# Attention scores: low-part products in 64 rows of the array, two heads or key halves to one score tile

## The chip, the cores and the metric

The kernel runs on one core of a Trainium2 chip. Its engines are TensorE (PE; its weight loads are listed apart as PEld), VectorE (DVE), ScalarE (ACT), GpSimd (POOL) and SyncE (SP), which issues the DMAs. Time is device microseconds of one execution. Before the change the median of three runs is 2173.24 us.

## The reference

Two layers of an encoder on two groups of tokens ("p": 1024 tokens, "s": 512), D = 1024, heads of 64. Every layer is a normalization, one input projection, three branches (convolution or attention), a gate, and one output projection. The attention parts, each query block of 128:

```python
# layer 0, sliding window of 3 blocks, with a sink
sc = einsum('bnqkgd,bnjkd->bnkgqj', qb, kb) * (d ** -0.5)
p = softmax(concatenate([where(mask, sc, NEG), sink_l], -1), -1)[..., :-1]
# layer 1, axial: 8 query heads on 2 key heads
p = softmax(einsum('bqkgd,bskd->bkgqs', qi, k) * scale, -1)
# layer 1, differential: 4 heads, two scores each
p = softmax(einsum('bqhd,bshd->bhqs', qi, k) * scale, -1).reshape(b, h, 2, 128, s)
a = p[:, :, 0] - lam * p[:, :, 1]
# both layers: 4 heads on 256 memory keys
p = softmax(einsum('bshd,bmhd->bhsm', q, mk) * (d ** -0.5), -1)
```

## The kernel before

**Split numbers.** Every fp32 operand of a product is kept as a high and a low part (fp32r). The projections make three products for each (`mm_a`, L309 to L311, 256 columns; `mm_b`, L323 to L325, 512 columns). Heads have 64 numbers, so q and k of a head are stored with the high parts in rows 0 to 63 and the low parts in rows 64 to 127. `load_q` (L568) makes two tiles: `qhh` with q's high part in both halves, `qll` with its low part in both.

**Scores.** `scores` (L578) makes two products of 128 rows into one PSUM bank: `qhh` by k (high by high and high by low, L579) and `qll` by k (low by high and low by low, L580). The score tiles "s" are a ring of two tiles of one bank, [128, 512] in fp32.

**Softmax.** DVE takes the negative maximum of a score tile (L675, L643 in the window attention), and ACT the exponential with a sum (L677, L650). For 1024 keys `head_softmax` (L681) works on two tiles of 512 keys with a maximum each, and then brings both to one: five small operations on DVE (L694, L696 to L699) and one on ACT (L695). The exponentials are then transposed on PE (128 columns each, four to a "pT" bank; L665, L731, L792, L863), split (`pt_split`), and multiplied by v. `swa` is the window attention (two heads to a step, W = 256 or 384 keys), `ax` the axial one, `diff` the differential one, `mem_attn` the memory one (four query blocks by 256 keys to a head, as two tiles of [128, 2, 256]).

**Order of the work.** The program is written stage by stage: projections of one group, then attention. A scheduler of the framework sets the order of each engine's instructions when the program is built. Attention is marked `urgent` (L189): it is put in as soon as the scheduler holds it ready, and projection products fill the rest of PE's queue. Each engine then runs its own list in that order, and waits where a buffer isn't free. `in_order` makes the slots of a ring go to tiles in program order. The ring "s" also serves the transposes of the first normalizations (`norm_steps(..., "s")`, L918 and L920). Key tiles are a ring of three ("k"), all DMAs go through SP's queue.

Of the kernel before, what the change touches and what calls it, by code (L numbers as in the profile page):

```python
# [45 lines left out]
def in_order(tc, chains):  # L46
    """Slots of a ring go to its tiles in the order of the program: the first writer of each tile is
    scheduled after that of the tile before it."""
# [20 lines left out]
def trunk_kernel(ctx: ExitStack, tc: tile.TileContext, a: dict, dbg=None):  # L69
# [8 lines left out]
    def ring(pool, shape, dt, tag, nm, stream=""):  # L78
        """a tile of a ring whose slots are taken in the order of the program (of its stream)"""
        t = pool.tile(shape, dt, tag=tag, name=nm, bufs=BUFS[tag])  # L80
        chains.setdefault((tag, stream), []).append(t)
        return t
# [27 lines left out]
    # ------------------------------------------------------------ constants  # L110
# [37 lines left out]
    # rotary tables with the gains folded in: cos * g and (signed) sin * g of the other half  # L148
# [14 lines left out]
    # ------------------------------------------------------------ scratch in DRAM  # L163
# [20 lines left out]
    # ------------------------------------------------------------ helpers  # L184
# [10 lines left out]
    def first(f):  # L195
        """what feeds the matrix products of the projections goes before the attention's work"""
        return f
        def g(*args, **kw):
            with tc.high_priority():
                return f(*args, **kw)  # L200
        return g
# [14 lines left out]
    def rstd(out, ss, mul, add):  # L216
        """out = (ss * mul + add) ** -0.5"""
# [71 lines left out]
    def load_act(src, pairs):  # L289
        """pairs of [128, 2, 512], hi and lo, of src [128, n, 512] in DRAM"""  # L290
# [10 lines left out]
    def mm_a(out, hs, sl, w, mid=None):  # L301
        """out[tok, cols] = act[:, sl].T @ w"""
# [12 lines left out]
    def mm_b(out, hs, w, csl, mid=None):  # L315
        """out[cols, tok] = w[:, csl].T @ act"""
# [17 lines left out]
    def stack_now():  # L334
        """the stack of the piece before"""
        while STACK:
            STACK.pop(0)()
# [9 lines left out]
    def between(keep=2):  # L347
        """one step of the work that goes between the projections' products"""
# [5 lines left out]
    def store_stack(t, nh, dst, h0, tok):  # L354
        """t [128, 2, nh, 64] (f32, SBUF): hi and lo, transposed, to dst[:, h0:h0+nh, tok:tok+256]"""
# [18 lines left out]
    def prep(ps, nh, dst, h0, tok, table=None, gain=None, query=False):  # L374
        """a q or k chunk ps [128, 2, nh, 64] (PSUM): rms norm (and a query's HD ** -0.5), gain, rotation"""
# [39 lines left out]
    def put_v(ps, nh, d, dst, t0, tag="stk"):  # L415
        """ps [128, 2, nh, d] (PSUM) to dst[:, 0:nh, t0:t0+2, 0:2d], hi | lo"""
# [10 lines left out]
    def silu2(ps, nm):  # L427
        """2 * silu of ps [128, 512]: ps * (1 + tanh(ps / 2))"""
# [5 lines left out]
    # ------------------------------------------------------------ input projection  # L434
# [9 lines left out]
    def in_proj(g, l, hs, ids, ahead=None, hfs=None):  # L444
        """hfs: the halves of the tokens (all of them if not given)"""
# [71 lines left out]
    def conv_cols(g, c, inner):  # L517
        """0.5 * conv along the tokens of inner; the halves follow one another"""
# [25 lines left out]
    # ------------------------------------------------------------ memory keys and values  # L544
# [22 lines left out]
    # ------------------------------------------------------------ attention  # L567
    def load_q(src, shape):  # L568
        """src(rows) -> AP of 64 rows; the hi rows twice and the lo rows twice"""
# [11 lines left out]

    def pt_split(ps):
# [7 lines left out]
    def fold(o, nm):  # L590
        """rows 64..127 of o [128, n] brought to rows 0..63, SBUF"""
# [5 lines left out]
    def finish_gqa(g, l, o, c0, tok):  # L597
        """o [128, 4, 128]: 4 heads of 128 queries; gated into y's column tiles c0, c0 + 1"""
# [10 lines left out]

    def load_kv(g, l, j):  # L610
        T = GROUPS[g]
        k = ring(sb, [128, 1024], F32R, "k", "k")[:, 0:T]
        dma(out=k, in_=S[g, l, "k", 0][:, j, :])
# [5 lines left out]
    def swa(g, j):  # L619
# [3 lines left out]
        for qt in range(nt):  # L623
# [6 lines left out]
            for hp in range(2):  # L630
# [3 lines left out]
                ss = []  # L634
                for i in range(2):
                    s = ring(psum, [128, 512], F32, "s", "s")[:, 0:W]
                    scores(s, [x[:, 2 * hp + i, :] for x in q2], k[:, b0 * 128:b1 * 128])
                    for side, cond, c0 in ((0, qt > 0, 0), (1, qt < nt - 1, W - 128)):
                        if cond:
                            nc.vector.tensor_tensor(  # L640
                                out=s[:, c0:c0 + 128], in0=s[:, c0:c0 + 128], in1=wmask[:, side, :], op=ALU.add
                            )
                    nc.vector.tensor_reduce(out=nm[:, i:i + 1], in_=s, axis=AXL.X, op=ALU.max, negate=True)  # L643
                    ss.append(s)
# [4 lines left out]
                for i in range(2):  # L649
                    nc.scalar.activation(  # L650
                        out=e[:, i, :], in_=ss[i], func=ACTF.Exp, bias=nm[:, i:i + 1], accum_out=su[:, i:i + 1],
# [21 lines left out]
    def softmax(s, e, su, nm):  # L673
        """s [128, n, w] (PSUM): nm [128, n] = -max, e [128, n, w] = exp(s + nm), su [128, n] the sums"""
# [6 lines left out]
    def head_softmax(q2, k, T, e):  # L681
        """one head, 128 queries: e [128, T]: exp(scores - max), with the max of each 512 columns;
        the result [128, T / 512]: what each 512 columns are to be multiplied by"""
        n = T // 512
        nm, su = smalla(n, "nm"), smalla(n, "su")
        for i in range(n):
            s = ring(psum, [128, 1, 512], F32, "s", "s")
            scores(s[:, 0, :], q2, k[:, i * 512:(i + 1) * 512])
            softmax(s, e[:, i * 512:(i + 1) * 512].unsqueeze(1), su[:, i:i + 1], nm[:, i:i + 1])
        if n == 1:  # L690
            nc.vector.reciprocal(out=su, in_=su)
            return su
        mn, f = smalla(1, "sk"), smalla(n, "sx")
        nc.vector.tensor_tensor(out=mn, in0=nm[:, 0:1], in1=nm[:, 1:2], op=ALU.min)  # L694
        nc.scalar.activation(out=f, in_=nm, func=ACTF.Exp, bias=mn, scale=-1.0)  # L695
        nc.vector.tensor_tensor(out=su, in0=su, in1=f, op=ALU.mult)  # L696
        nc.vector.tensor_tensor(out=mn, in0=su[:, 0:1], in1=su[:, 1:2], op=ALU.add)
        nc.vector.reciprocal(out=mn, in_=mn)
        nc.vector.tensor_tensor(out=f, in0=f, in1=mn.to_broadcast([128, n]), op=ALU.mult)  # L699
        return f  # L700

    @urgent
    def ax(g, j):
        T = GROUPS[g]
        nt = T // 128
        per = 1024 // T
        k, v = load_kv(g, 1, j)
        for qt in range(nt):
# [3 lines left out]
            for hp in range(2):  # L712
                es = []
                for i in range(2):
                    if i % per == 0:
                        e2 = et("e")
                    e = e2[:, (i % per) * T:(i % per + 1) * T]
                    h = 4 * j + 2 * hp + i
                    f = head_softmax([x[:, 2 * hp + i, :] for x in q2], k, T, e)
                    for n in range(T // 512):  # L720
                        c = e[:, n * 512:(n + 1) * 512]
                        nc.gpsimd.tensor_scalar(
                            out=c, in0=c, scalar1=f[:, n:n + 1], scalar2=0.5, op0=ALU.mult, op1=ALU.mult
# [383 lines left out]
```

## Time and profile before

| | |
|---|---|
| three runs | 2166.95, 2173.24, 2174.95 us |
| profiled execution, span from first to last instruction | 2165.8 us (the page gives no other time of it) |
| mean granted TensorE clock | 0.988 |
| busy: PE, PEld, DVE, ACT, POOL | 96%, 88%, 71%, 55%, 50% |
| score products on PE | 1024: 320 + 320 of 512 keys, 64 + 64 of 384, 128 + 128 of 256 |

PE's rows give a start and a length for each product. Products overlap, so what one costs in a full queue is the distance from its start to the next start, not its length. The distances are read from the timeline.

### The profile page before, as it was taken

What the parts mean: (1) busy time and instruction counts of PE and PEld (TensorE: products, weight loads), DVE (VectorE), ACT (ScalarE), POOL (GpSimd) and SP (SyncE); (2) the same over time, 40 slices, a digit from 0 to 9 for tenths busy, and PEclk for the clock granted to TensorE, in tenths of its full rate; (3) what the DMA queues carried; (4) which work ended last, traced back from release to release, by engine and by line L of the source; (5) the groups of instructions that cost most, each with busy time, mean ns of one, the idle gap of its engine ahead of it and who ended that gap; (6) DMA issues with size and microseconds to landing.
All of it is one profiled execution on the core that took longest, in us unless ns stands there. A gap on an engine that the chain in (4) does not pass through costs nothing. (4 is left out here: it accounts for less than half of the span.)

```text
span 2165.8 us, 41192 instructions
## 1 busy us (share of the span) xinstructions
PE 2080.9 (96%) x14336; PEld 1916.8 (88%) x14336; DVE 1547.2 (71%) x3264; ACT 1189.7 (55%) x2838; POOL 1075.9 (50%) x1134
## 2 busy tenths in 40 slices
PE   6999999999999999999999989997998999999999
PEld 6988978889999999999998878886997899998999
DVE  8768877745445687877988886777778877875652
ACT  5545633453334566766766655546466666764441
POOL 6845532342225674853855574332346686842331
PEclk9999999999999999999999999998999999999999
DMA  6675463436776522443345565447475566567753
GB/s 229 193 214 169 140 210 106 115 100 212 250 234 220 174 84 88 131 129 114 94 121 180 165 194 166 122 147 229 143 213 179 167 186 203 175 204 217 227 169 105
DMA packets 317408, 363.74 MB, mean 168 GB/s; under 512 B 25360, under 2 KB 222736, under 8 KB 317200
## 3 DMA queue, kind: packets, MB, share of 16 engines
q1 hardware_dynamic: 317200, 361.10, 54.6%
q8 instruction: 114, 1.87, 0.4%
q14 instruction: 94, 0.77, 0.1%
HBM read 261.38 MB, written 99.61 MB: 167 GB/s over the span
## 5 line engine op out<-in xcount | busy, mean ns | idle before, releaser
L187 POOL TENSOR_TENSOR wlo<-wraw,whi 128x512 fp32r<-128x512 f32 x182 | 249.3, 1371 | 322.9 <-ACT whi L186 285.0
L186 ACT CAST whi<-wraw 128x512 fp32r<-128x512 f32 x388 | 237.3, 621 | 254.8 <-PE po L311 74.9
L677 ACT ACTIVATE e<-s,nm 128x512 f32<-128x512 f32 (+1 forms) x416 | 264.4, 640 | 173.4 <-DVE nm L675 124.5
L675 DVE TENSOR_REDUCE nm<-s 128x1 f32<-128x512 f32 (+1 forms) x368 | 248.0, 681 | 37.7 <-PE s L580 36.2
L587 DVE TENSOR_TENSOR ptlo<-pT,pthi 128x512 fp32r<-128x512 f32 x352 | 238.0, 683 | 42.6 <-ACT pthi L586 40.9
L586 ACT CAST pthi<-pT 128x512 fp32r<-128x512 f32 x352 | 201.1, 588 | 118.1 <-PE pT L665 48.4
L309 PE MATMUL po<-whi,ahi 128*128 128x256 f32 x896 | 254.7, 285 | 1.7 <-DVE xr L900 1.4
L310 PE MATMUL po<-wlo,ahi 128*128 128x256 f32 x896 | 254.0, 284 | 0.0
L311 PE MATMUL po<-whi,alo 128*128 128x256 f32 x896 | 253.5, 284 | 0.5 <-DVE alo L187 0.4
L187 DVE TENSOR_TENSOR wlo<-wraw,whi 128x512 fp32r<-128x512 f32 x206 | 175.9, 855 | 105.1 <-ACT whi L186 104.4
L309 PE MATMUL pa<-whi,ahi 128*128 128x256 f32 x768 | 221.2, 288 | 4.0 <-DVE z L431 2.1
L311 PE MATMUL pa<-whi,alo 128*128 128x256 f32 x768 | 221.3, 288 | 0.0
L310 PE MATMUL pa<-wlo,ahi 128*128 128x256 f32 x768 | 221.2, 288 | 0.0
L223 POOL TENSOR_TENSOR rs<-ss,mhalf 128x8 f32<-128x8 f32 (+2 forms) x108 | 141.7, 1313 | 149.7 <-DVE ss L219 141.6
L579 PE MATMUL s<-k,qhh 128*128 128x512 f32 (+2 forms) x512 | 194.6, 385 | 17.2 <-ACT e L677 10.6
L580 PE MATMUL s<-k,qll 128*128 128x512 f32 (+2 forms) x512 | 185.5, 367 | 2.6 <-DMA qll<-st_p1dq 1.6
L309 PEld LDWEIGHTS po<-whi,ahi 128*128 128x128 f32 x896 | 171.1, 191 | 3.7 <-DVE xr L900 1.8
L311 PEld LDWEIGHTS po<-whi,alo 128*128 128x128 f32 x896 | 171.1, 191 | 2.0 <-DVE alo L187 0.9
L310 PEld LDWEIGHTS po<-wlo,ahi 128*128 128x128 f32 x896 | 171.3, 191 | 1.3
L324 PE MATMUL pb<-h,whi 128*128 128x512 f32 x432 | 171.6, 397 | 0.0
L325 PE MATMUL pb<-h,wlo 128*128 128x512 f32 x432 | 171.4, 397 | 0.0
L323 PE MATMUL pb<-h,whi 128*128 128x512 f32 x432 | 170.9, 396 | 0.0
(171 smaller groups left out, 6272.9 us busy)
## 6 DMA issues: line engine op xcount, KB each, us to landing
wraw<-in_w_in_dram SPq DMA_DIRECT2D x252, 256.0 KB, 3.1
wraw<-in_w_out_dram SPq DMA_DIRECT2D x120, 256.0 KB, 3.4
alo<-y_p SPq DMA_DIRECT2D x20, 512.0 KB, 5.0
zg_p<-z SPq DMA_DIRECT2D x32, 256.0 KB, 3.0
k<-st_p1dk SPq DMA_DIRECT2D x14, 512.0 KB, 4.4
v<-dv_p SPq DMA_DIRECT2D x14, 512.0 KB, 5.4
zg<-zg_p SPq DMA_DIRECT2D x48, 128.0 KB, 2.7
y_p<-yo SPq DMA_DIRECT2D x48, 128.0 KB, 2.6
```

The costliest lines, as they stand in the source:

```text
L186: nc.scalar.copy(out=out_hi, in_=src)
L187: lo_eng.tensor_tensor(out=out_lo, in0=src, in1=f32(out_hi), op=ALU.subtract)
L309: nc.tensor.matmul(out=out, lhsT=h, rhs=wh, start=(k == 0), stop=False)
L310: nc.tensor.matmul(out=out, lhsT=h, rhs=wl, start=False, stop=False)
L311: nc.tensor.matmul(out=out, lhsT=l_, rhs=wh, start=False, stop=(k == n - 1))
L324: nc.tensor.matmul(out=out, lhsT=wh, rhs=l_, start=False, stop=False)
L579: nc.tensor.matmul(out=out, lhsT=q2[0], rhs=k, start=True, stop=False)
L580: nc.tensor.matmul(out=out, lhsT=q2[1], rhs=k, start=False, stop=True)
L586: nc.scalar.copy(out=hi, in_=ps)
L587: nc.vector.tensor_tensor(out=lo, in0=ps, in1=f32(hi), op=ALU.subtract)
L675: nc.vector.tensor_reduce(out=nm, in_=s, axis=AXL.X, op=ALU.max, negate=True)
L677: nc.scalar.activation(out=e[:, j, :], in_=s[:, j, :], func=ACTF.Exp, bias=nm[:, j:j + 1], accum_out=su[:, j:j + 1],)
```

## The change

- `scores2` fills one score tile of two banks, [128, 2, 512], one bank for each of two heads (window attention, and the 512-token group) or for each half of 1024 keys. It makes two products of 128 rows with `qhh` as before, then two products of 64 rows: q's low part by k's high part, the first in rows 0 to 63, the second in rows 64 to 127 of the array. The products of low by low parts are left out.
- For the second one, k's high part must lie in rows 64 to 127. `load_k` with `swap` loads the two halves of k the other way round, in two DMAs. The window attention now takes two tiles of the ring "k" for a key head, where it took one; for 1024 keys one tile holds the first half as stored and the second half swapped. The program issues 1604 DMAs, where it issued 1556.
- The ring "s" has one tile, of two banks, where it had two of one bank.
- A score tile has one maximum over [128, 2, W], [128, 1024] or [128, 2, 512], and the window's mask is added for both heads at once. For 1024 keys the five small operations on DVE and the one on ACT go, and one reciprocal of [128, 1] is left.
- `mem_attn` keeps its 128-row products, with one score tile [128, 4, 256] to a head.

```diff
-    "s": 2, "t": 2, "x": 1, "d": 2, "o": 1,
+    "s": 1, "t": 2, "x": 1, "d": 2, "o": 1,
...
+    def scores2(s, qs, ks):
+        for i in range(2):
+            nc.tensor.matmul(out=s[:, i, :], lhsT=qs[i][0], rhs=ks[i], start=True, stop=False)
+        for i in range(2):
+            r = slice(64 * i, 64 * i + 64)
+            nc.tensor.matmul(out=s[:, i, :], lhsT=qs[i][1][r], rhs=ks[i][r], start=False, stop=True)
+
+    def load_k(k, src, swap):
+        if not swap:
+            dma(out=k, in_=src)
+            return
+        for r in range(2):
+            dma(out=k[64 * r:64 * r + 64], in_=src[64 - 64 * r:128 - 64 * r])
...
+    def load_k2(src, T):
+        k = ring(sb, [128, 1024], F32R, "k", "k")
+        load_k(k[:, 0:512], src[:, 0:512], False)
+        load_k(k[:, 512:1024], src[:, T - 512:T], True)
+        return k[:, 0:512], k[:, 512:1024]
...
     def load_kv(g, l, j):
         T = GROUPS[g]
-        k = ring(sb, [128, 1024], F32R, "k", "k")[:, 0:T]
-        dma(out=k, in_=S[g, l, "k", 0][:, j, :])
+        src = S[g, l, "k", 0][:, j, :]
+        if l:
+            k = load_k2(src, T)
+        else:
+            k = []
+            for i in range(2):
+                k.append(ring(sb, [128, 1024], F32R, "k", "k")[:, 0:T])
+                load_k(k[i], src, i == 1)
...
-                ss = []
-                for i in range(2):
-                    s = ring(psum, [128, 512], F32, "s", "s")[:, 0:W]
-                    scores(s, [x[:, 2 * hp + i, :] for x in q2], k[:, b0 * 128:b1 * 128])
...
-                    nc.vector.tensor_reduce(out=nm[:, i:i + 1], in_=s, axis=AXL.X, op=ALU.max, negate=True)
-                    ss.append(s)
+                s = ring(psum, [128, 2, 512], F32, "s", "s")[:, :, 0:W]
+                scores2(
+                    s, [[x[:, 2 * hp + i, :] for x in q2] for i in range(2)],
+                    [x[:, b0 * 128:b1 * 128] for x in k],
+                )
+                for side, cond, c0 in ((0, qt > 0, 0), (1, qt < nt - 1, W - 128)):
+                    if cond:
+                        nc.vector.tensor_tensor(
+                            out=s[:, :, c0:c0 + 128], in0=s[:, :, c0:c0 + 128],
+                            in1=wmask[:, side, :].unsqueeze(1).to_broadcast([128, 2, 128]), op=ALU.add,
+                        )
+                nc.vector.tensor_reduce(out=nm, in_=s, axis=AXL.X, op=ALU.max, negate=True)
...
-    def head_softmax(q2, k, T, e):
-        n = T // 512
-        nm, su = smalla(n, "nm"), smalla(n, "su")
-        for i in range(n):
-            s = ring(psum, [128, 1, 512], F32, "s", "s")
-            scores(s[:, 0, :], q2, k[:, i * 512:(i + 1) * 512])
-            softmax(s, e[:, i * 512:(i + 1) * 512].unsqueeze(1), su[:, i:i + 1], nm[:, i:i + 1])
-        if n == 1:
-            nc.vector.reciprocal(out=su, in_=su)
-            return su
-        mn, f = smalla(1, "sk"), smalla(n, "sx")
-        nc.vector.tensor_tensor(out=mn, in0=nm[:, 0:1], in1=nm[:, 1:2], op=ALU.min)
-        nc.scalar.activation(out=f, in_=nm, func=ACTF.Exp, bias=mn, scale=-1.0)
-        nc.vector.tensor_tensor(out=su, in0=su, in1=f, op=ALU.mult)
-        nc.vector.tensor_tensor(out=mn, in0=su[:, 0:1], in1=su[:, 1:2], op=ALU.add)
-        nc.vector.reciprocal(out=mn, in_=mn)
-        nc.vector.tensor_tensor(out=f, in0=f, in1=mn.to_broadcast([128, n]), op=ALU.mult)
-        return f
+    def two_softmax(qs, ks, es):
+        n = len(es)
+        s = ring(psum, [128, 2, 512], F32, "s", "s")
+        scores2(s, qs, ks)
+        sv = s.rearrange("p a k -> p (a k)").rearrange("p (n k) -> p n k", n=n)
+        nm, su = smalla(n, "nm"), smalla(n, "su")
+        nc.vector.tensor_reduce(out=nm, in_=sv, axis=AXL.X, op=ALU.max, negate=True)
+        for j in range(n):
+            nc.scalar.activation(
+                out=es[j], in_=sv[:, j, :], func=ACTF.Exp, bias=nm[:, j:j + 1], accum_out=su[:, j:j + 1],
+            )
+        nc.vector.reciprocal(out=su, in_=su)
+        return [su[:, j:j + 1] for j in range(n)]
+
+    def softmax_pair(q2s, kk, T):
+        if T == 1024:
+            es = [et("e") for _ in range(2)]
+            fs = []
+            for i in range(2):
+                fs += two_softmax([q2s[i]] * 2, kk[i], [es[i]])
+        else:
+            eb = et("e")
+            es = [eb[:, i * T:(i + 1) * T] for i in range(2)]
+            fs = two_softmax(q2s, [kk[i][i] for i in range(2)], es)
+        return es, fs
...
-                    for t2 in range(0, 4, 2):
-                        s = ring(psum, [128, 2, 256], F32, "s", "s")
-                        for t in range(2):
-                            scores(s[:, t, :], [x[:, (t2 + t) * 128:(t2 + t + 1) * 128] for x in q2], k2[:, i, :])
-                        qt = 4 * qb + t2
-                        softmax(s, e[:, t2:t2 + 2, :], su[:, t2:t2 + 2], smalla(2, "nm"))
+                    s = ring(psum, [128, 4, 256], F32, "s", "s")
+                    for t in range(4):
+                        scores(s[:, t, :], [x[:, t * 128:(t + 1) * 128] for x in q2], k2[:, i, :])
+                    softmax(s, e, su, smalla(4, "nm"))
```

The scheduler makes a new order. Three places of it follow.

**PE, axial attention, group p.** `s` is a score tile, `pa` a projection of 256 columns, `o` the product with v. Before, with two products to each tile of 512 keys:

```order
L579 MATMUL s<-k,qhh 128x512
L580 MATMUL s<-k,qll 128x512
L310 MATMUL pa<-wlo,ahi 128x256
L311 MATMUL pa<-whi,alo 128x256
L309 MATMUL pa<-whi,ahi 128x256
L579 MATMUL s<-k,qhh 128x512
L580 MATMUL s<-k,qll 128x512
```

and in the changed kernel, where L587 are the 128-row products and L590 those of 64 rows:

```order
L311 MATMUL pa<-whi,alo 128x256
L309 MATMUL pa<-whi,ahi 128x256
L587 MATMUL s<-k,qhh 128x512 x2
L590 MATMUL s<-k,qll 128x512 x2
L310 MATMUL pa<-wlo,ahi 128x256
```

The four products of 1024 keys now stand together. From L590 here to the next L587, 36 rows on, the order has 34 products of 256 columns and 8 transposes. Of the 208 pairs of 64-row products, 198 stand side by side like this; in the other 10 something stands between the two.

**PE, memory attention of layer 0, group s.** `pT` are transposes, `o` the product with v of 512 columns. Before, two tiles that follow each other:

```order
L579 MATMUL s_18726<-k_18702,qhh_18709 128x256
L580 MATMUL s_18726<-k_18702,qll_18712 128x256
L865 MATMUL o_18616<-pthi_18622,v_18580 128x512
L579 MATMUL s_18774<-k_18702,qhh_18766 128x256
L580 MATMUL s_18774<-k_18702,qll_18769 128x256
...
L865 MATMUL o_18616<-ptlo_18623,v_18580 128x512
```

and in the changed kernel, the end of one tile (L579 and L580 are its last two of eight products) and the start of the next:

```order
L579 MATMUL s_17515<-k_17446,qhh_17507 128x256
L580 MATMUL s_17515<-k_17446,qll_17510 128x256
L891 MATMUL pT_17482<-ident_r_66,e_17459 128x128
L891 MATMUL pT_17493<-ident_r_66,e_17459 128x128
...
L893 MATMUL o_17481<-pthi_17487,v_17448 128x512
L893 MATMUL o_17481<-ptlo_17488,v_17448 128x512
L893 MATMUL o_17481<-pthi_17498,v_17448 128x512
L893 MATMUL o_17481<-ptlo_17499,v_17448 128x512
L579 MATMUL s_17579<-k_17564,qhh_17571 128x256
```

Between two tiles of two banks stand the eight transposes and four products of the head before, and nothing of a projection.

**DVE, axial attention.** Before, the small operations of one head, and the maximum that follows:

```order
L694 TENSOR_TENSOR sk<-nm 128x1
L696 TENSOR_TENSOR su<-su,sx 128x2
L697 TENSOR_TENSOR sk<-su 128x1
L698 RECIPROCAL sk<-sk 128x1
L699 TENSOR_TENSOR sx<-sx,sk 128x2
L675 TENSOR_REDUCE nm<-s 128x1
```

and now, with L721 the maximum over 1024 keys and L726 the reciprocal:

```order
L388 TENSOR_TENSOR raw<-raw,rs 128x512
L721 TENSOR_REDUCE nm<-s 128x1
L726 RECIPROCAL su<-su 128x1
L605 TENSOR_TENSOR ptlo<-pT,pthi 128x512 x2
L721 TENSOR_REDUCE nm<-s 128x1
```

The five small operations between two maxima became one.

## Rows read from the trace of the kernel before

**Rows 1.** The page: its first line and the busy time of each engine.

```profile
span 2165.8 us, 41192 instructions
PE 2080.9 (96%) x14336; PEld 1916.8 (88%) x14336; DVE 1547.2 (71%) x3264; ACT 1189.7 (55%) x2838; POOL 1075.9 (50%) x1134
```

**Rows 2.** What TensorE (PE) waited for: total us, times, longest us.

```profile
PE s L579 <- ACT e L677: 10.6, 11, 2.4
```

**Rows 3.** Two stretches: span, busy us of each engine (xcount), granted clock, DMA share, GB/s.

```profile
756.00:810.00 54.00, 54.00 (x395) 50.62 (x394) 46.18 (x104) 36.49 (x88) 40.71 (x46) 1.00 0.28 84
1458.00:1512.00 54.00, 42.03 (x209) 33.11 (x209) 40.09 (x98) 35.65 (x100) 12.82 (x22) 0.87 0.78 227
```

**Rows 4.** The largest group of PE's low-part score products.

```profile
L580 PE MATMUL s<-k,qll 128*128 128x512 f32 x320 | 128.6, 402 | 1.6 <-DMA qll<-st_p1dq 1.6
```

**Rows 5.** PE in order of time in an axial stretch: start us, us, instruction.

```profile
835.86 0.60 PE L731 MATMUL pT<-ident_r,e 128*128 128x128 f32 x4
836.21 0.36 PE L310 MATMUL pa<-wlo,ahi 128*128 128x256 f32 x1
836.41 0.28 PE L311 MATMUL pa<-whi,alo 128*128 128x256 f32 x1
836.53 0.28 PE L309 MATMUL pa<-whi,ahi 128*128 128x256 f32 x1
...
838.39 0.40 PE L579 MATMUL s<-k,qhh 128*128 128x512 f32 x1
838.62 0.40 PE L580 MATMUL s<-k,qll 128*128 128x512 f32 x1
838.86 0.28 PE L311 MATMUL pa<-whi,alo 128*128 128x256 f32 x1
```

**Rows 6.** PE in order of time in a sliding-window stretch.

```profile
322.38 0.34 PE L580 MATMUL s<-k,qll 128*128 128x384 f32 x1
322.55 0.40 PE L324 MATMUL pb<-h,whi 128*128 128x512 f32 x1
```

**Rows 7.** PE's weight loads (PEld) in order of time, axial stretch.

```profile
838.27 0.19 PEld L579 LDWEIGHTS s<-k,qhh 128*128 128x128 f32 x1
838.39 0.19 PEld L580 LDWEIGHTS s<-k,qll 128*128 128x128 f32 x1
```

**Rows 8.** Groups on VectorE (DVE), shapes kept apart.

```profile
L675 DVE TENSOR_REDUCE nm<-s 128x1 f32<-128x512 f32 x320 | 216.1, 681 | 32.4 <-PE s L580 31.3
L643 DVE TENSOR_REDUCE nm<-s 128x1 f32<-128x384 f32 x64 | 33.7, 547 | 0.5
L696 DVE TENSOR_TENSOR su<-su,sx 128x2 f32<-128x2 f32 x128 | 35.1, 274 | 35.6 <-ACT sx L695 25.9 <-ACT e L677 9.5
```

**Rows 9.** One score tile in the axial stretch and the next in its bank.

```profile
837.68 0.39 PE L580 MATMUL s<-k,qll 128*128 128x512 f32 x1
838.11 0.69 DVE L675 TENSOR_REDUCE nm<-s 128x1 f32<-128x512 f32 x1 [0.26 <-PE s L580]
838.90 0.69 ACT L677 ACTIVATE e<-s,nm 128x512 f32<-128x512 f32 x1 [0.61 <-DVE nm L675]
839.48 0.19 ACT L677 ACTIVATION_READ_ACCUMULATOR e<-s,nm 128x1 f32 x1
...
842.38 0.48 PE L579 MATMUL s<-k,qhh 128*128 128x512 f32 x1
```

**Rows 10.** PE in the memory attention: first products of the first and the eighth tile.

```profile
1479.49 0.56 PE L579 MATMUL s<-k,qhh 128*128 128x256 f32 x1 [0.22 <-ACT e L650]
...
1493.55 0.36 PE L579 MATMUL s<-k,qhh 128*128 128x256 f32 x1
```

**Rows 11.** ACT there: two exponentials of one tile.

```profile
1485.39 0.49 ACT L677 ACTIVATE e<-s,nm 128x256 f32<-128x256 f32 x1
1485.86 0.48 ACT L677 ACTIVATE e<-s,nm 128x256 f32<-128x256 f32 x1
```

**Rows 12.** DMA issues of one kind of key tile: count, KB each, median us to landing.

```profile
k<-st_p1dk SPq DMA_DIRECT2D x14, 512.0 KB, 4.4
```

More of the change, by code (lines that the diff above doesn't have):

```diff
@@ L633, in swa @@
                 ns = nsink[:, h0:h0 + 2]
-                ss = []
-                for i in range(2):
-                    s = ring(psum, [128, 512], F32, "s", "s")[:, 0:W]
-                    scores(s, [x[:, 2 * hp + i, :] for x in q2], k[:, b0 * 128:b1 * 128])
[L638 to L642, printed above, removed]
-                    nc.vector.tensor_reduce(out=nm[:, i:i + 1], in_=s, axis=AXL.X, op=ALU.max, negate=True)
-                    ss.append(s)
+                s = ring(psum, [128, 2, 512], F32, "s", "s")[:, :, 0:W]
[10 more added lines that the diff above has]
+                nc.vector.tensor_reduce(out=nm, in_=s, axis=AXL.X, op=ALU.max, negate=True)
                 nc.vector.tensor_tensor(out=nm, in0=nm, in1=ns, op=ALU.min)
@@ L650, in swa @@
                     nc.scalar.activation(
-                        out=e[:, i, :], in_=ss[i], func=ACTF.Exp, bias=nm[:, i:i + 1], accum_out=su[:, i:i + 1],
+                        out=e[:, i, :], in_=s[:, i, :], func=ACTF.Exp, bias=nm[:, i:i + 1], accum_out=su[:, i:i + 1],
                     )
@@ L705, in ax @@
         nt = T // 128
-        per = 1024 // T
         k, v = load_kv(g, 1, j)
@@ L712, in ax @@
             for hp in range(2):
[L713 to L721, printed above, removed]
+                es, fs = softmax_pair([[x[:, 2 * hp + i, :] for x in q2] for i in range(2)], [k, k], T)
+                for e, f in zip(es, fs):
+                    for c in (e[:, n * 512:(n + 1) * 512] for n in range(T // 512)):
                         nc.gpsimd.tensor_scalar(
-                            out=c, in0=c, scalar1=f[:, n:n + 1], scalar2=0.5, op0=ALU.mult, op1=ALU.mult
+                            out=c, in0=c, scalar1=f, scalar2=0.5, op0=ALU.mult, op1=ALU.mult
                         )
-                    es.append(e)
                 for kc in range(nt // 2):
@@ L746, in diff @@
         nt = T // 128
-        per = 1024 // T
         ks = []
         for i in range(2):
-            k = ring(sb, [128, 1024], F32R, "k", "k")[:, 0:T]
-            dma(out=k, in_=S[g, 1, "dk", hd // 2][:, 2 * (hd % 2) + i, :])
-            ks.append(k)
+            src = S[g, 1, "dk", hd // 2][:, 2 * (hd % 2) + i, :]
+            if T == 1024:
+                ks.append(load_k2(src, T))
+            else:
+                k = ring(sb, [128, 1024], F32R, "k", "k")[:, 0:T]
+                load_k(k, src, i == 1)
+                ks.append((k, k))
         vs = []
@@ L767, in diff @@
                 qt = 2 * qp2 + t
-                e2, fs = [], []
-                for i in range(2):
-                    if i % per == 0:
-                        eb = et("e")
-                    e = eb[:, (i % per) * T:(i % per + 1) * T]
-                    fs.append(head_softmax(
-                        [x[:, i, t * 128:(t + 1) * 128] for x in q2], ks[i], T, e,
-                    ))
-                    e2.append(e)
+                e2, fs = softmax_pair(
+                    [[x[:, i, t * 128:(t + 1) * 128] for x in q2] for i in range(2)], ks, T
+                )
                 for n in range(T // 512):
@@ L779, in diff @@
                     nc.gpsimd.tensor_scalar(
-                        out=c1, in0=c1, scalar1=fs[1][:, n:n + 1], scalar2=lamb, op0=ALU.mult, op1=ALU.mult
+                        out=c1, in0=c1, scalar1=fs[1], scalar2=lamb, op0=ALU.mult, op1=ALU.mult
                     )
                     nc.vector.scalar_tensor_tensor(
-                        out=c0, in0=c0, scalar=fs[0][:, n:n + 1], in1=c1, op0=ALU.mult, op1=ALU.subtract
+                        out=c0, in0=c0, scalar=fs[0], in1=c1, op0=ALU.mult, op1=ALU.subtract
                     )
```

## The prediction

> **What bounds the kernel now.** I read the page's busy times first, then what PE waits for, then the stretches, then the products one by one. PE is busy for 2080.9 of 2165.8 us; no other engine comes over 71%, if PE's own weight loads are left aside [rows 1]. Its idle time is 84.9 us in all, and the score products' wait for a free bank is a small part of it: 10.6 us in 11 waits [rows 2]. The stretches show two regimes. In the axial stretch PE has no idle time at all, because projection products lie between the pieces of attention; in the stretch from 1458 us, where attention has little projection work beside it, PE is busy for 42.0 of 54 us and its mean granted clock falls to 0.87 [rows 3]. So almost everywhere a microsecond of PE's queue that goes is a microsecond of the kernel, and in a few tens of microseconds the length of the attention's own chain counts instead.
>
> What a product costs is the distance between starts: 0.12 us for 256 columns and 0.23 to 0.24 for 512 [rows 5], 0.17 for 384 [rows 6]. The record of a 512-column product is 0.40 us long [rows 4, 5], so about 0.17 us of it lies under the next one.
>
> **The change, part by part.**
>
> *Low-part products.* Of the 512 low-part products, 96 belong to the memory attention and stay. The other 416 become 208 pairs: 160 of 512 columns, 32 of 384, 16 of 256. If the two of a pair run at the same time, a pair costs one distance instead of two. At best the second starts with the first: 160 x 0.235 + 32 x 0.17 + 16 x 0.12 = 45.0 us saved. At worst, if they overlap, the second starts one weight load behind the first; weight loads stand 0.12 us apart [rows 7], which leaves 160 x 0.115 + 32 x 0.05 + 0 = 20.0 us. No row shows two products at once, so nothing tells where between these it lies; I take the middle, 32.5 us. Ten of the 208 pairs have other work between their products and are counted as lost: 32.5 x 198/208 = 31 us, all of it on the path, since it is PE's queue.
>
> The Trainium skill, "TensorE: Matmul & The Clock Gate", section "Measured speedup vs the span model", says that products in different row groups start some 4 ns apart. By that page the saving would be about 44 us, and the time, as an estimate, 2136 us instead of the 2149 below; no run here shows it yet.
>
> *The switch between 128-row and 64-row products.* Each pair needs one switch there and one back, 416 in all; the trace has none. The nearest thing in it is the switch between transposes and products. Four transposes and the product behind them take 0.55 us from the first start to the start after (835.86 to 836.41); with 0.12 for the product that leaves 0.11 for each transpose, no more than a weight load [rows 5, 7]. That switch costs nothing that can be seen, so I take 0. The other end is an array that must run empty first: 0.17 us, the part of a record that otherwise lies under the next product, and 0.12 more if the weight load has to wait too. A gain from the switch I can exclude, since it adds a condition and removes no work. This end is a rival below.
>
> *One score tile where there were two.* The next tile's first product now waits for the last exponential of the tile before it. Rows 9 show what one tile takes: 1.99 us from its last product's start (837.68) to the end of its exponential (839.67), and its bank is used again 2.71 us later. For 1024 keys the maximum grows with its columns, 0.134 us for each 128 (from 0.547 to 0.681 us [rows 8]), to 1.22 us, 0.54 more; and a second exponential of 0.77 us follows [rows 9]. That is 3.3 us. The new order puts 34 products of 256 columns and 8 transposes between two tiles there: 34 x 0.12 + 8 x 0.11 + 0.235 = 5.2 us. The wait is covered with 1.9 us to spare.
>
> It isn't covered in the stretch from 1458 us. In the memory attention eight tiles start within 14.06 us [rows 10], seven steps, so 4.0 us to a head. One tile to a head makes a chain: eight products (0.84 us to the last start), 0.3 until the maximum, 1.22, 0.1, four exponentials 0.47 us apart [rows 11] for 1.9, and 0.1: 4.5 us, of which nothing overlaps with the next head's. That is 0.5 us for each of four heads, 2 us at least. The ceiling comes from the whole new order, priced with the distances above: 24 of the 231 gaps between tiles hold under 4 us of PE work, nearly all of them in this stretch; if each were filled up to 4 us with waiting it would be 49 us, of which some 12 are idle time that is already there [rows 3], so 37. I take 6, near the lower end, because the window attention held both its banks until its last exponential before, too.
>
> *The start.* The first sixteen transposed blocks of the normalizations pass through the same ring, now one tile at a time, each held for one 512-column operation of DVE, about 0.68 us [rows 8]. If all were exposed it would be 11 us. DVE does its next step on the same block meanwhile, and PE's transposes fit in beside that; I take 1.
>
> *DVE and ACT.* For each of 128 heads' blocks, five small operations of about 0.27 us [rows 8] become one reciprocal, and two maxima become one: some 1.1 + 0.15 us of 128 x 1.25 = 160 us, a tenth of DVE's time. DVE isn't the bound, so I count 0. If PE's waits shorten with it, that would be a gain of up to 10 us, an eighth of PE's idle time.
>
> *Loads of k.* 48 DMAs more in SP's queue. A key tile lands 4.4 us after its issue [rows 12] and is issued a stage ahead. In the window attention two of the ring's three tiles now belong to one key head, so the second head's second copy is loaded only when the first head is done. Projection work covers that in group p: 0. Without cover it costs one landing for each such head, two heads, 9 us, in the high end.
>
> **Sum.** The profiled execution spans 2165.8 us, and the page gives no other time of it; the median of the three runs is 7.4 us above that, 0.3%. Against the median: 2173.2 - 31 + 6 + 1 = **2149 us**, 1.1% less. The measurement tells about 0.5% from no change, 11 us here: 2162 and 2184 are the marks.
>
> **The rivals.**
>
> *The switch empties the array.* Every one of the 416 switches then costs 0.17 us on PE: 71 us, and the time is 2149 + 71 = 2220; with the weight loads waiting too, 50 us more, 2270. This turns the sign once a switch costs over 24/416 = 0.058 us, a third of what the record leaves. For it: the 64-row products use another division of the array, which the transposes don't. Against it: the transposes' switch is free [rows 5]. The Trainium skill, "TensorEngine Tiling (Array Packing)", section "Key Properties", says just this: changing the tiling mode drains TensorE. By that page this rival would be the forecast, and no run here shows it yet. Chance 0.27.
>
> *The pairs don't overlap.* The second 64-row product waits for the first, as any product does today. Then nothing is saved, and 2173 + 7 = 2180 us. Speaking for it: there isn't one pair of products in this trace that ran at once. Chance 0.12.
>
> *The single score tile binds.* The waits of the thin stretch come out near their ceiling, with part of the start exposed: 30 to 48 us instead of 7, so 2172 to 2190. For it: PE already idles for 12 us there, and waits for DVE and ACT queue behind other work. Against it: the slack of 1.9 us elsewhere, and less work on DVE. Chance 0.13.
>
> *The forecast*, pairs overlap at a cheap switch: 0.48, with its own range from 2126 (45 us saved, waits as now, and a few us from DVE) to 2165.
>
> **How the numbers follow.** Faster by over 0.5%: the forecast but for its upper edge, 0.46. Within 0.5%: that edge 0.02, most of the pairs that don't overlap 0.09, most of the single tile 0.08, a switch of 0.06 to 0.08 us 0.02: 0.21. Slower: the dearer switches 0.25, and 0.08 from the other two: 0.33. The range goes from 2126, the best pairs, to 2224, the emptied array with its 0.17 us; beyond lie the dearer switch, 0.09, and some 0.09 more on both sides.
>
> **What would show it.** In PE's timeline of the changed kernel: L590's second product at most 0.12 us behind the first, the next 128-row product 0.23 us behind the second, and no gap between the last L587 and the first L590 beyond 0.24. A gap of 0.4 or more at both borders is the emptied array; 0.23 between the two L590 is no overlap. Waits of L587 on ACT's exponential far over today's 10.6 us, outside the thin stretch too, are the single tile. The maximum should read 1.2 us, and DVE's busy time some 1390 us. I would be wrong altogether if PE's idle time grew outside these places, by the new order alone.

## The result and the profile after

The changed kernel takes 2237.75 us (median of 4 runs, 2237.17 to 2242.96), the kernel before 2170.09 in the same comparison: a ratio of 1.032, 95% interval 1.0296 to 1.0344. It is 68 us slower, where 2149 us, 1.1% less, had been forecast. The page of the changed kernel, to be held against [rows 1]:

```profile
span 2235.4 us, 39938 instructions
PE 2141.3 (96%) x14336; PEld 1882.8 (84%) x14336; DVE 1422.1 (64%) x2408; ACT 1135.5 (51%) x2454; POOL 1086.4 (49%) x1134
```

DVE and ACT got relief (125 and 54 us less busy), and no gain of it shows. PE makes the same 14336 products and is busy 60 us longer; its idle time is 94.1 us after 84.9. So of the 70 us by which the span grew, most lies in how long the products take. PE's timeline shows one pair of 512 columns (start us, us, instruction, count of products in the row):

```profile
803.03 0.61 PE L587 MATMUL s<-k,qhh 128*128 128x512 f32 x2
803.58 0.50 PE L590 MATMUL s<-k,qll 64*128 64x512 f32 x2
804.01 0.50 PE L323 MATMUL pb<-ahi,whi 128*128 128x512 f32 x1
804.35 0.40 PE L324 MATMUL pb<-alo,whi 128*128 128x512 f32 x1
804.58 0.39 PE L325 MATMUL pb<-ahi,wlo 128*128 128x512 f32 x1
```

The two 64-row products of L590 lie in 0.50 us together: they start 3 ns apart (median of the 153 pairs of 512 columns that stayed together), so they do overlap. But both borders are dear. From the second L587 (0.22 behind the first) to the pair it takes 0.33 us instead of 0.23, from the pair to the next 128-row product 0.43, and from that to the one after it 0.34. PE's weight loads of the same pair show what goes with the last one:

```profile
803.58 0.18 PEld L590 LDWEIGHTS s<-k,qll 64*128 64x128 f32 x2 [0.35 <-issue]
804.01 0.19 PEld L323 LDWEIGHTS pb<-ahi,whi 128*128 128x128 f32 x1 [0.24 <-issue]
804.11 0.19 PEld L324 LDWEIGHTS pb<-alo,whi 128*128 128x128 f32 x1
```

Elsewhere a weight load stands one product ahead of its product [rows 5, 7]; L323's at 804.01 comes with it, and L324's only 0.11 us later. Over all pairs the medians say the same: 0.09 us too much going in, 0.20 coming out, 0.11 behind, 0.40 us for the round trip (into the 64-row division of the array and back), against 0.23 saved by the overlap (512 columns). That is a loss of 0.17 us for each of 160 pairs, and by the same medians 0.23 for 32 pairs of 384 columns and 0.28 for 16 of 256: 39 of the 68 us.

The largest piece of the rest shows in one stretch. PE's groups of lines from 1485 to 1555 us (columns: instruction and count | busy us, mean ns | idle us before) hold attention alone; not one projection product stands among them. Three of them:

```profile
L697 PE MATMUL pT<-ident_r,e 128*128 128x128 f32 x40 | 10.0, 382 | 0.7 <-DVE yo L854 0.6 <-DVE e L688 0.2
L587 PE MATMUL s<-k,qhh 128*128 128x256 f32 (+2 forms) x18 | 6.6, 459 | 7.7 <-ACT e L682 6.1 <-ACT e L723 1.6
L579 PE MATMUL s<-k,qhh 128*128 128x256 f32 x16 | 6.3, 404 | 2.1 <-ACT e L682 1.6 <-ACT e L709 0.5
```

The same stretch as a window (span, busy us of PE, PEld, DVE, ACT, POOL, granted clock, DMA share, GB/s), and before's stretch without projection products:

```profile
1485.00:1555.00 70.00, 50.66 (x199) 35.12 (x200) 47.06 (x114) 31.82 (x96) 13.86 (x22) 0.71 0.51 141
```

```profile
1471.00:1506.00 35.00, 24.83 (x113) 18.88 (x113) 23.62 (x57) 20.99 (x66) 9.54 (x19) 0.80 0.89 248
```

Without filling, PE is busy 7 us in 10, and the clock falls to its lower level, 1.2 GHz, for part of the time. This bare stretch was 36 us long before (from the end of the last projection product to the next one's start) and is 71 us long now. In both kernels the same 6348 projection products stand ahead of it, but of PE's other products 3015 instead of 3130: more attention is left for it. The changed kernel comes to it 14 us later than the kernel before and leaves it 49 us later. The mean granted clock of the whole execution went from 0.988 to 0.978.

### The profile page after: what moved, and what is told of

The parts are those of the page before. It is cut to its first block, busy times and chain, and to the rows that moved or that the text cites. A ratio compares the mean times of both kernels' runs of the same rounds, so it can differ in the third digit from the quotient of the medians.

```text
span 2235.4 us, 39938 instructions
## 1 busy us (share of the span) xinstructions
PE 2141.3 (96%) x14336; PEld 1882.8 (84%) x14336; DVE 1422.1 (64%) x2408; ACT 1135.5 (51%) x2454; POOL 1086.4 (49%) x1134
## 4 chain that ended last, share of the span: by engine, by line
PE 81%; DMA 7%; DVE 5%; ACT 2%; issue 2%; POOL 2%; SPq 0%; ACTq 0%; POOLq 0%; DVEq 0%
PE pb L323 7%; PE pb L325 7%; PE pb L324 7%; PE pa L309 7%; PE pa L310 7%; PE pa L311 6%; PE po L309 4%; PE po L311 4%; PE po L310 4%; PE s L587 4%; PE s L590 4%; PE o L768 4%; PE pT L764 3%; PE stT L366 2%; PE pT L822 1%
## 5 line engine op out<-in xcount | busy, mean ns | idle before, releaser
L723 ACT ACTIVATE e<-s,nm 128x1024 f32<-128x1024 f32 (+1 forms) x192 | 186.5, 973 | 189.1 <-DVE nm L721 182.4
L605 DVE TENSOR_TENSOR ptlo<-pT,pthi 128x512 fp32r<-128x512 f32 x352 | 233.5, 684 | 76.7 <-ACT pthi L604 74.9
L604 ACT CAST pthi<-pT 128x512 fp32r<-128x512 f32 x352 | 196.6, 590 | 132.2 <-PE pT L697 52.7
L721 DVE TENSOR_REDUCE nm<-s 128x1 f32<-128x1024 f32 (+1 forms) x160 | 194.9, 1218 | 68.2 <-PE s L590 67.4
L756 POOL TENSOR_SCALAR e<-e,su 128x512 f32<-128x512 f32 x160 | 121.1, 770 | 142.7 <-DVE su L726 136.4
L324 PE MATMUL pb<-h,whi 128*128 128x512 f32 x432 | 172.5, 399 | 0.0
L323 PE MATMUL pb<-h,whi 128*128 128x512 f32 x432 | 172.4, 399 | 0.0
L309 PE MATMUL pa<-whi,h 128*128 128x256 f32 x576 | 165.8, 288 | 0.4 <-ACT raw L377 0.4
```

What stands on the lines that cost most here:

```text
L309: nc.tensor.matmul(out=out, lhsT=h, rhs=wh, start=(k == 0), stop=False)
L323: nc.tensor.matmul(out=out, lhsT=wh, rhs=h, start=(k == 0), stop=False)
L324: nc.tensor.matmul(out=out, lhsT=wh, rhs=l_, start=False, stop=False)
L604: nc.scalar.copy(out=hi, in_=ps)
L605: nc.vector.tensor_tensor(out=lo, in0=ps, in1=f32(hi), op=ALU.subtract)
L721: nc.vector.tensor_reduce(out=nm, in_=sv, axis=AXL.X, op=ALU.max, negate=True)
```

## The experiments

All ratios are to the kernel before in the same comparison, with 95% intervals.

### The tile alone

```diff
-        for i in range(2):
-            nc.tensor.matmul(out=s[:, i, :], lhsT=qs[i][0], rhs=ks[i], start=True, stop=False)
-        for i in range(2):
-            r = slice(64 * i, 64 * i + 64)
-            nc.tensor.matmul(out=s[:, i, :], lhsT=qs[i][1][r], rhs=ks[i][r], start=False, stop=True)
+        for i in range(2):
+            scores(s[:, i, :], qs[i], ks[i])
```

and k loaded as before, in one DMA.

> The single score tile of two banks with its one maximum, the changed order of the rest and the joined exponentials, but every score product over 128 array rows and k loaded unswapped in one DMA. Theory A (a round trip between the 128-row and the 64-row division costs 0.40 us against 0.23 us that the pair saves, so 39 us come from the pairs, and the other 28 from the single tile and the lower clock behind it): about 2198 us, 2187 to 2210, with windows of the thin stretch (from 1458 us) again below 46 us of PE time. Theory B (all 68 us come from the borders of the pairs): 2170, within 0.5% of before. Theory C (all come from the single tile and the order, the pairs are neutral): 2238.

Measured: 2198.42 us, ratio 1.014 (1.0097 to 1.0182). Theory A's number. The page:

```profile
span 2199.1 us, 39942 instructions
PE 2096.1 (95%) x14336; PEld 1927.0 (88%) x14336; DVE 1418.7 (65%) x2408; ACT 1129.7 (51%) x2454; POOL 1096.2 (50%) x1134
```

The tile costs some 29 us and the pairs the other 39 (2237.75 less 2198.42); the interval leaves 21 to 39 us for the tile. That the pairs' 39 us are also what the distances gave is partly chance: against this run the changed kernel's PE is busy 45 us longer and idle 9 us less, and its bare stretch is longer too. The same products as in the kernel before now leave PE idle for 103.0 us, 18 more, and the bare stretch is 54 us long.

### The pair alone

```diff
-    "s": 1, "t": 2, "x": 1, "d": 2, "o": 1,
+    "s": 2, "t": 2, "x": 1, "d": 2, "o": 1,
...
-            nc.tensor.matmul(out=s[:, i, :], lhsT=qs[i][1][r], rhs=ks[i][r], start=False, stop=True)
+            nc.tensor.matmul(out=s[i], lhsT=qs[i][1][r], rhs=ks[i][r], start=False, stop=True)
```

with two one-bank tiles, and the maxima and rescaling of before.

> The products of the low parts in pairs of 64 rows, but into two score tiles of one bank each as in the kernel before, with a maximum per 512 keys, the small rescaling operations and the memory heads of before. Theory A: about 2209 us, 2197 to 2222 (before plus 160 x 0.171 + 32 x 0.23 + 16 x 0.278 = 39 us). Theory B: 2238. Theory C: 2139 to 2170, since the pairs would then save 31 us or nothing.

Measured: 2298.04 us, ratio 1.0591 (1.0552 to 1.0629). No theory gave that, since the edit did more than was meant. With two tiles the scheduler pulled the couples apart; in PE's timeline one 64-row product stands alone:

```profile
832.60 0.48 PE L587 MATMUL s<-k,qhh 128*128 128x512 f32 x1
833.01 0.50 PE L590 MATMUL s<-k,qll 64*128 64x512 f32 x1
833.43 0.50 PE L325 MATMUL pb<-ahi,wlo 128*128 128x512 f32 x1
```

Only 28 of 208 pairs stayed together, and there are 388 round trips instead of 218. PE's busy time rose by 149 us over before, 0.38 us to a round trip, though the run couldn't isolate the pair. In this program it was the single tile that kept the pairs together.

### The same rows, and a single switch

In the changed kernel, both products in rows 0 to 63 (k loaded unswapped), and apart from that the order of the four products:

```diff
-            r = slice(64 * i, 64 * i + 64)
+            r = slice(0, 64)
```

```diff
         for i in range(2):
             nc.tensor.matmul(out=s[:, i, :], lhsT=qs[i][0], rhs=ks[i], start=True, stop=False)
-        for i in range(2):
             r = slice(64 * i, 64 * i + 64)
```

> The changed kernel with both 64-row products in array rows 0 to 63, k unswapped, DMAs counted as in the changed kernel. If the overlap of the two products is real, they now stand 0.23, 0.175 and 0.12 us apart (512, 384, 256 columns): 160 x 0.23 + 32 x 0.175 + 16 x 0.12 = 45 us more than the changed kernel, about 2282 us (2270 to 2295). If the 3 ns between their starts in the records hide a serial execution: 2238.

> The changed kernel with its four products in the order 128 rows, 64 rows, 128 rows, 64 rows: no overlap and two round trips between the divisions to a pair instead of one. Theory A (0.40 us to a round trip of 512 columns, as between the rows): the changed kernel plus 45 us for the lost overlap plus 208 x 0.40 = 83 us, about 2366 us (2340 to 2390). If the borders are not paid per switch but belong to the overlapped pair: about 2283 or less.

Measured: 2269.52 us, ratio 1.0461 (1.0414 to 1.0509), and 2327.59 us, ratio 1.0729 (1.0679 to 1.0779). The first is just below its range, the second 12 us below Theory A's and 45 us above the other one. PE's timeline of the single switch:

```profile
816.49 0.39 PE L587 MATMUL s<-k,qhh 128*128 128x512 f32 x1
816.81 0.50 PE L589 MATMUL s<-k,qll 64*128 64x512 f32 x1
817.24 0.49 PE L587 MATMUL s<-k,qhh 128*128 128x512 f32 x1
817.66 0.49 PE L589 MATMUL s<-k,qll 64*128 64x512 f32 x1
818.09 0.50 PE L323 MATMUL pb<-ahi,whi 128*128 128x512 f32 x1
```

One 64-row product takes 0.43 us to the next 128-row product, exactly what the pair took: the second product of a pair is free, the overlap real. Against the tile alone this kernel has 416 round trips and nothing else of weight. PE's busy time rose by 156.0 us, 0.375 to a round trip; the time rose by only 129 us, as PE's idle time fell by 31. With two products in the same rows, PE's timeline reads:

```profile
807.43 0.61 PE L587 MATMUL s<-k,qhh 128*128 128x512 f32 x2
807.97 0.73 PE L590 MATMUL s<-k,qll 64*128 64x512 f32 x2
808.63 0.50 PE L323 MATMUL pb<-ahi,whi 128*128 128x512 f32 x1
808.97 0.40 PE L324 MATMUL pb<-alo,whi 128*128 128x512 f32 x1
```

The second stands 0.34 us behind the first, the step out takes 0.32, and the next distance is 0.34 again (medians). So both borders are alike: 0.09 us too much at the step, and 0.11 behind the first product after it; in the pair, where the second product starts with the first, the 0.11 of the step in shows on the way out. The round trip is 0.40 us here too, and the pair takes 0.23 us more than the overlapped one. PE's busy time says the same: 43 us more than in the changed kernel (2184.7 after 2141.3), about the 45 expected. The time rose by only 32 us, because PE's idle time fell by 10.5 (83.6 after 94.1).

### One tile, cut in other ways

In the tile-alone kernel: a maximum to each bank everywhere; a lasting tile so that banks come free singly; this and a maximum to a sliding-window head, or to a memory half.

```diff
-        s = ring(psum, [128, 2, 512], F32, "s", "s")
+        s = s_tile
```

> All score products over 128 rows, one tile of two banks as in the tile-alone run, but each bank gets its own maximum, exponentials and rescaling as in the kernel before; only the release of the two banks stays joint. Theory S (the 30 us of the single tile come from the joint release: the next tile's first product waits for the last exponential of both banks): 2190 to 2205 us. Theory M (they come from the one maximum, which starts only after the last product of both banks and takes 1.2 us): within 0.5% of before, about 2170.

> As the tile-alone run with its one maximum everywhere, but the two banks are one lasting tile, so that a new product waits only for the readers of the bank that it writes. Theory S: a good part comes back, 2175 to 2190 us. Theory M: as the tile-alone run, 2193 to 2203.

> As the run with release by bank, and the sliding-window heads also get a mask and a maximum per head again, as in the kernel before; axial, differential and memory heads keep one maximum. Theory W (the loss sits in the sliding-window tail of the thin stretch at 1458 us, where the profile of the tile-alone run shows waits of 6.4 us for the exponentials and 4.4 us for the scaled ones): 2168 to 2180 us, and less idle time in 1458 to 1566 us than the 22 us of the tile-alone run. Theory H (it sits in the memory heads, as the prediction had priced): no better than the run with release by bank.

> As the run with release by bank, and the memory heads get a maximum per half again; the sliding-window heads keep one maximum for two heads. Theory H: 2168 to 2180 us. Theory W: as the run with release by bank, within 6 us.

Measured: 2542.66 us (ratio 1.173, 1.1712 to 1.1747), 2198.29 (1.0135, 1.012 to 1.015), 2277.92 (1.0514, 1.0496 to 1.0532) and 2201.46 (1.0151, 1.0136 to 1.0166). By the numbers the first fits neither theory, the second M, the third H and the fourth W. But none of them tests what it was meant to, and the waits of PE tell why (total us, times, longest). In the first, and in the second between 1476 and 1482 us:

```profile
PE s L579 <- ACT e L700: 93.7, 78, 2.3
```

```profile
PE s L579 <- ACT e L676: 3.3, 1, 3.3
```

The framework orders readers and writers by whole tiles here. A product into bank 1 waits for the exponential of bank 0, and a new tile's product waited until the second exponential was done (the wait ends at 1478.46, that exponential runs from 1477.74 for 0.57 us). So the lasting tile changed nothing, and cutting the softmax in two made the halves serial. What is left is how dear it is to make heads serial: 3 us for the memory heads, 80 for the sliding-window heads.

### The waits alone, on the kernel before

The kernel before, with its tiles and operations, and waits added by family of heads (`wr` and `rd` are a tile's writers and readers in program order; the second wait needs the scores of both tiles written ahead of the first maximum):

```diff
+        tc.add_manual_dep(wr[seq[i + 2]][0][1], rd[seq[i + 1]][-1][1].name, sync, reason="joint")
+        if f in M_FAMS:
+            tc.add_manual_dep(use[1], last[1].name, sync, reason="joint")
```

> The kernel before, with its own two score tiles, operations and 128-row products, and only added waits: the first product of every second score tile also waits for the last exponential of the tile before it (both banks come free together), the first mask or maximum of a couple of tiles waits for the last product of the second (except in the 512-key heads), and the normalisation tiles at the start, which use the same ring, follow one another singly. Theory J (the 29 us of the single tile are these waits): 2190 to 2206 us. Theory O (they come from the joined maximum, the missing small operations or another order): below 2180.

> The kernel before with these waits in the sliding-window heads alone. Theory W (the largest part sits in the sliding-window tail of the thin stretch): 2179 to 2190 us, with the gain in idle time and lost clock between 1458 and 1566 us. Theory H (it sits in the memory heads, as the prediction had priced): within 4 us of before.

> The kernel before with these waits in the memory heads alone. Theory W: within 4 us of before (24 heads, most of them covered). Theory H: 2179 to 2190 us.

> The kernel before with the added wait at the normalisation tiles of the start alone (24 of them take the ring of the score tiles). By the idle time of the first 108 us, which rose by 7 us in the tile-alone run: 2174 to 2180 us. If the start is covered as the prediction took it: within 2 us of before.

> The kernel before with the waits of a joint tile in the axial and differential heads alone. Theory X (what the start, the window and the memory heads leave of the 40 us of all waits together, 40 - 14 - 0 - 3 = 23, sits here): 2185 to 2195 us. Theory Y (these heads are covered, as the prediction took it, and the parts only add up to more together): within 5 us of before, 2161 to 2171.

> The waits in the axial and differential heads and at the start together. Theory X with independent parts: 2198 to 2210 us. Theory Y: about 2180, as the start alone.

> The waits in the sliding-window heads and at the start together. Theory X: about 2180, as the start alone. Theory Y with the window's tail binding once the start is late: 2190 us or more.

> As the run with the waits in the axial and differential heads, but only the joint release: a maximum may start as soon as its own tile's products are done. If the release is what costs: 2183 to 2192 us. If the late start of the first maximum does: within 5 us of before.

| waits in | us | ratio, 95% interval | bare stretch, us |
|---|---|---|---|
| all | 2206.34 | 1.0177 (1.0158 to 1.0196) | 55 |
| sliding window | 2166.34 | 0.9998 (0.9983 to 1.0012) | 36 |
| memory | 2169.19 | 1.0010 (0.9998 to 1.0023) | 31 |
| start | 2179.82 | 1.0050 (1.0036 to 1.0064) | 36 |
| axial and differential | 2187.11 | 1.0095 (1.0069 to 1.0121) | 60 |
| these and start | 2199.63 | 1.0167 (1.0140 to 1.0193) | 59 |
| sliding window and start | 2176.51 | 1.0051 (1.0033 to 1.0070) | 34 |
| axial and differential, release only | 2181.51 | 1.0076 (1.0058 to 1.0095) | 55 |

Theories W and H fall: neither the sliding-window nor the memory heads cost what was lost, though the lost time shows up beside them. Theory J stands, with a time 0.3 us above its range, and so does Theory X. Waits alone cost 40 us, more than the tile's 29; the axial and differential heads carry 20 of it and the start 14, and together they give 33. Of the 20, 15 come from the joint release; the other 5 can't be told from nothing, since the two intervals overlap. The tile-alone kernel is 8 us faster than all the waits, perhaps by the relief on DVE and ACT; no run isolates that.

How waits in the axial heads cost time elsewhere is in the last column. The run with waits in the axial and differential heads, from 1455 us:

```profile
1455.00:1514.00 59.00, 44.53 (x176) 32.94 (x177) 42.04 (x120) 31.46 (x94) 12.18 (x22) 0.71 0.64 177
```

Its bare stretch is 60 us long, where the runs of the table without these waits have 31 to 36. The added waits are part of what the scheduler works with. Here too 6348 projection products stand ahead of the stretch, as in the kernel before, but 67 fewer of PE's other products (3063 instead of 3130): beside the same filling less attention gets done, and more is left to run bare. The run comes to its bare stretch 16 us earlier than the kernel before (1454.5 after 1470.5) and leaves it 8 us later (1514.0 after 1506.4); the rest of the loss comes behind it and was not located. Of the 18 us by which the whole span is longer, 6 are idle time of PE and 11 are busy time: the same 14336 products take longer, and the mean granted clock is 0.981 instead of 0.988. Why the scheduler orders it so was not tested by itself; the counts are what the trace shows.

### Three tiles at the start

```diff
-            ps = ring(psum, [128, 4, 128], F32, banks, "hT")
+            ps = ring(psum, [128, 4, 128], F32, banks[(2 * t + q) % len(banks)], "hT")
```

with "sso" for "s", so that every third transposed block of the first normalizations takes the idle bank of "o".

> The kernel before, where every third normalisation tile at the start takes the bank of the attention output, which is idle there: three slots instead of two. If the slots still bind at two: 2155 to 2164 us, faster than both kernels. If the first 108 us wait for loads and VectorE by then: within 0.5% of before.

Measured: 2163.17 us, ratio 0.9985 (0.997 to 0.9999), no difference beyond what can be told. Two slots are enough there, one is not. Its bare stretch is 42 us long after 36, so a small gain at the start may have been lost there; that was not tested. No version tried beats the kernel before by more than that.

## Why the prediction was wrong

**Low-part products: right in kind, too cautious in size.** The prediction took the middle between 20 and 45 us. The second product starts with the first (3 ns), which is the best end: 45.0 x 198/208 = 43 us. The Trainium skill, "TensorE: Matmul & The Clock Gate", "Measured speedup vs the span model", gives some 4 ns for each further product of a packed group, and the trace agrees; the prediction's 44 us by that page had left in the ten pairs that are pulled apart. That ten of the 208 pairs would be pulled apart was right too.

**The switch: the step that failed.** The switch between 128-row and 64-row products was priced at 0, after the switch between transposes and products [rows 5], and taken as a rival at 0.17 us, 0.29 with the weight load. Measured: 0.375 us of PE's busy time to a round trip, 0.19 to a switch; with 218 round trips that is 82 us. The transposes use the array in the same division as the products (128*128 in the rows of both), so their switch was the wrong neighbour, as the rival's own argument said. The rival "the switch empties the array" fits what the rows show, and its turn point of 0.058 us to a switch is passed threefold. Of its two parts, 0.17 and 0.12 us, neither comes in full at the step: there 0.09 is lost, and 0.11 behind it, where the weight load isn't one product ahead. The sign named for it, 0.4 us at both borders, shows on the way out (0.43) but not on the way in (0.33), and no run separates emptying the array from waiting for the weight load. The Trainium skill, "TensorEngine Tiling (Array Packing)", "Key Properties", says that changing the tiling mode drains TensorE, and the trace fits that: the product behind a border starts 0.07 us before the record in front of it ends (median of the 512-column pairs), where some 0.17 us lie under the next one in a full queue. These ends are modelled.

**One score tile: 6 us taken, in the wrong place.** "The wait is covered with 1.9 us to spare" was worked out for one axial stretch, and the direct waits bear it out: L587 waits 12 us for exponentials in all, about what [rows 2] show. But the waits of the axial and differential heads cost 20 us all the same, by the order and the longer bare stretch. The prediction's last sentence named a way of being wrong that is near this one (idle time by the new order alone) and gave it no price; more than half of the loss is longer products, not idle time. The 6 us for the memory heads were too many, if anything: 3, which can't be told from nothing.

**The start: 1 us taken, 14 measured.** The ring holds 24 of the transposed blocks, not sixteen: a third normalization uses it (L927). At 0.68 us each that would be 16 us if all were exposed, and 14 were lost. The first 108 us show 6 us less PE busy time in that run; the rest was not located.

**DVE and ACT, DMAs: near.** The maximum takes 1.22 us (1218 ns in the profile), as worked out; DVE is busy 1422 us, where 1390 had been worked out, so its relief is 125 us instead of 160. That it counts for little fits the times, but no run isolates it. PE waits 0.8 us for key tiles in all.

**The sum with measured terms:** 2170.1 - 43 + 82 + 29 = 2238, against 2237.75. The forecast's sum had the same form; one term at zero and one in the wrong place made the difference. That the two agree within 1 us is luck: the tile's term alone is known only to some 9 us, and 82 us is busy time, part of which less idle time makes up for.

## What to carry to other kernels

Price a change of the array's division by itself before counting on packed rows: here a round trip cost 0.37 to 0.40 us and one pair of 512 columns gave back 0.23, so by these numbers it takes two pairs or more to a round trip before the packing pays (not tried here). A wait that is covered where it stands can still cost: here less attention got done beside the same filling, and more was left for the stretch without any, so look at the stretch with the least filling, not only at the wait. And before believing an experiment with half a buffer, read in the trace that the halves came free singly.

## What the runs showed that was not expected

The second 64-row product in the same rows stood 0.34 us behind the first instead of 0.23, and leaving from it took 0.32 us instead of 0.43, so that a round trip costs the same 0.40 us with and without the overlap. PE idled 31 us less when its own products got slower (the single switch against the tile alone), so a fifth of the added product time was hidden. And one slot instead of two for 24 short-lived tiles at the start cost 14 us, while a third slot gave nothing that can be told.
